# relu(h)² on ScalarE in place of VectorE, and the first w2 tiles in the first product's weight pool

## The chip, the cores and the metric

The kernel runs on one core of one Trainium2 chip. The metric is the device time of one execution in microseconds (us). Five engines work side by side, each through its own instructions in order: TensorE (PE in the profile; PEld is its weight load), VectorE (DVE), ScalarE (ACT), GpSimd (POOL) and SyncE (SP), whose queue issues nearly all DMAs of the part that matters here.

## The reference, cut to what matters

One encoder layer on x of 2048 tokens x 1024: differential attention and a retention scan, mixed into x, then a feed-forward part with a hidden width of 4096.

```
h = rms_norm(x, norm2_g)
u = relu(h @ w_mlp1)          # 2048 x 1024 @ 1024 x 4096
x = x + (u * u) @ w_mlp2      # 2048 x 4096 @ 4096 x 1024
```

Everything ahead of these three lines is the same in both kernels.

## The kernel before, in words

Both ff products are cut into 2 x 2 blocks and computed with seven block products in place of eight (Strassen-Winograd): sums and differences of blocks are formed first, and the results are added up afterwards. Each fp32 operand is split into a high and a low part (`split_sbuf`: the high part by a ScalarE copy on L44, the low part by a VectorE subtraction on L50), and each product is three matmuls, L36 high·high, L37 and L38 with one low part each (`mm3`).

**First ff product.** It goes over two halves of the tokens (`g`), and in each over eight blocks of the hidden width (`blk`). One block (`winograd_block`) runs its seven products in the order b11, b21, t2, t1, t3, b22, t4 (named after the token operand, which lies in SBUF for the whole half). One product is 24 matmuls into two banks `ps`, one for each `s`, so a block is 168 matmuls. The weight side is a raw w1 tile, or a sum of such tiles made by GpSimd on L238 (`comb`, tag `s`, three buffers in pool `wp`): s2 for the product t2, s1 for t1, s3 for t3, s4 for b22. s2 is made from s1. Their splits are `wh` and `wl`, three buffers each. VectorE adds the banks up on L279 into tiles `c`, and each finished tile goes to `consume`: relu(h)² on L1419, a store to DRAM on L1413 (`put`), and from each four tiles four sums on GpSimd (L1417, `comb` inside `consume`), eight a block, which are stored too. In the first half, blocks 1 to 4 are each followed by `fill_units`, which turns and splits a quarter of the second half's tokens: here blocks 2 to 5 run beside that work, and they are called fill blocks below.

**Second ff product.** Seven products p1, p2, p6, p7, p5, p3, p4 follow, each of eight chunks; a chunk is 48 matmuls into eight banks `p`. A chunk needs `ra` (the stored hidden units, L1490, split into `ah` and `al`) and a w2 tile (`br`, 512 KB, L1464, split into `wh` and `wl`). The w2 tiles lie in pool `bp` ("m2b"), four buffers. The pools of this stage (`ap`, `bp`, `cpool`) are opened when the pool `hp` of the first stage is closed, and lie in its place, in the order in which they are opened; a tile there can be loaded when what lay there has been read for the last time.

**What sets the order.** The program is written out for one stage after the other, and a scheduler with a timeline of its own puts each engine's instructions in order at build time. So a change in one place can move instructions on all engines. A DMA on SP whose wait isn't over holds up all that stand behind it on SP.

Of the kernel before, what the change touches and what calls it, by code (L numbers as in the profile page):

```python
# [8 lines left out]
F32 = mybir.dt.float32  # L9
F32R = mybir.dt.float32r  # L10
F16 = mybir.dt.float16
AF = mybir.ActivationFunctionType
ALU = mybir.AluOpType
# [4 lines left out]
P = 128  # L18
# [58 lines left out]
H = G // 2  # L77
# [12 lines left out]
def winograd_units(nc, pool, saved=None, units=UNITS, issued=None, places=None):  # L90

    tb = {n: [pool.tile([P, 4, H], F32R, tag=f"{n}{hl}", name=f"{n}{hl}", bufs=1) for hl in "hl"] for n in places or units}
    if saved is not None:
        for n in units:
            for t, d in zip(tb[n], saved[n]):
                e = nc.gpsimd if issued is not None and n in ("t1",) else nc.sync
                ins = e.dma_start(t[:].bitcast(F32), d[:].rearrange("p (k t) -> p k t", k=4).bitcast(F32))
                if issued is not None:
                    issued.append(ins)
    return tb  # L100
# [424 lines left out]
def pool(tc, name, bufs, space=None, side=None):  # L525
    kw = {} if space is None else dict(space=space)
    return tc.tile_pool(name=name, bufs=bufs, side=side, reuse_waits="tile", **kw)
# [3 lines left out]
def encoder(ctx: ExitStack, tc: tile.TileContext, a: dict, out: bass.AP, dbg=None):  # L531
    nc = tc.nc
    x, w_in, w_out, w1, w2 = a["x"], a["w_in"], a["w_out"], a["w_mlp1"], a["w_mlp2"]
    x = x.rearrange("b s d -> (b s) d")
    out = out.rearrange("b s d -> (b s) d")
# [110 lines left out]
    def load_half(pool, w, c):  # L646
        r = pool.tile([P, KT, 256], F32, tag="raw", name="raw")
        nc.sync.dma_start(r[:], w[:, c : c + 256].rearrange("(k p) n -> p k n", p=P))
        return [r]

    def load_w(pool, w, c0):

        return [r for fh in range(2) for r in load_half(pool, w, c0 + fh * 256)]
# [7 lines left out]
    with ExitStack() as ph:  # L661
        wp = ph.enter_context(pool(tc, "wst", 3))
# [93 lines left out]
        first = load_w(wp, w_in, blocks[0][1] * 512)  # L756
# [117 lines left out]
        for g in range(S // G):  # L874
            if g:
                first = load_w(wp, w_in, blocks[0][1] * 512)
# [276 lines left out]
    with ExitStack() as ph:  # L1153
# [50 lines left out]
        for i in range(LT, NI):  # L1204
# [20 lines left out]
            if i == NI - 4:  # L1225
# [4 lines left out]
                for n in ("vh", "vl"):  # L1230
                    t = ap2.tile([P, 2, DM], F32, tag=n, name="wos")
# [59 lines left out]
    with ExitStack() as ph:  # L1291
# [5 lines left out]
        t = ep.tile([P, 2, DM], F32, tag="raw", name="wos")  # L1297
# [46 lines left out]
        for i in range(NT + 2):  # L1344
# [6 lines left out]
            if i == 12:  # L1351
                first = [r for fh in range(2) for r in load_half(ep, w1, fh * (DFF // 2))]
                tb0 |= winograd_units(nc, ep, saved[1], UNITS[1:2])
                t = ep.tile([P, 2, 4, 256], F32R, tag="raw", name="w0")
# [16 lines left out]
    wp = mlp.enter_context(pool(tc, "m1w", 3))  # L1371
    pp = mlp.enter_context(pool(tc, "ps_m1", 8, PSUM))

    def load_w1(blk):
        return [r for fh in range(2) for r in load_half(ep, w1, fh * (DFF // 2) + blk * 256)]

    with ExitStack() as ph:
        hp = ph.enter_context(pool(tc, "h2T", 1))
        for g in range(S // G):
            if g:  # L1380
                first = load_w1(0)
                tb0 = winograd_units(nc, ep, saved[2], UNITS[:2])
            loads = []
            tb = tb0 | winograd_units(nc, hp, saved[1 + g], UNITS[2:], loads, ("t4", "b22", "t3", "t2", "t1"))
            for blk in range(DFF // 512):
                if ahead:
                    hl = [wp.tile([P, 4, 256], F32R, tag=f"w{n}", name=f"w{n}") for n in "hl"]
                    split_sbuf(nc, hl[0][:], hl[1][:], first[0][:, 4:8], "act", "dve")
                    ahead["a12"] = hl
                    sums = [wp.tile([P, 4, 256], F32, tag="s", name="s") for _ in range(2)]  # L1390
                    nc.gpsimd.tensor_tensor(out=sums[0][:], in0=first[1][:, 0:4], in1=first[1][:, 4:8], op=ALU.add)
                    nc.gpsimd.tensor_tensor(out=sums[1][:], in0=sums[0][:], in1=first[0][:, 0:4], op=ALU.subtract)
                    hl = [wp.tile([P, 4, 256], F32R, tag=f"w{n}", name=f"w{n}") for n in "hl"]
                    split_sbuf(nc, hl[0][:], hl[1][:], sums[1][:], "act", "dve")
                    ahead["s2"] = hl
                    sums = dict(s1=sums[0][:], s2=sums[1][:])
                else:
                    sums = {}
                if blk == 0:
                    raws = first  # L1400
                elif blk == 1:
                    with tc.issue_after(loads[-1].ins):
                        raws = load_w1(blk)
                else:
                    raws = load_w1(blk)

                us = [{} for _ in range(2)]

                def consume(t, fh, th, s):
                    u, f0 = us[s], blk * 256 + s * P  # L1410

                    def put(n):
                        nc.sync.dma_start(ua_d[n][f0 : f0 + P, g * H : (g + 1) * H], u[n][:])  # L1413

                    def comb(n, x0, x1, op, o=None):
                        u[n] = wp.tile([P, H], F32, tag="d", name="c", bufs=BUFS["d"]) if o is None else o
                        nc.gpsimd.tensor_tensor(out=u[n][:], in0=u[x0][:], in1=u[x1][:], op=op)  # L1417

                    nc.vector.scalar_tensor_tensor(  # L1419
                        out=t[:], in0=t[:], scalar=0.0, in1=t[:], op0=ALU.max, op1=ALU.mult  # L1420
                    )
                    n = f"a{th + 1}{fh + 1}"
                    u[n] = t
                    if n == "a21":
                        comb("s1", "a21", "a22", ALU.add)
                        put("s1")
                        comb("s3", "a11", "a21", ALU.subtract, t)
                        put("s3")
                        comb("s2", "s1", "a11", ALU.subtract)
                        put("s2")  # L1430
                    else:
                        put(n)
                    if n == "a12":
                        comb("s4", "a12", "s2", ALU.subtract)
                        put("s4")

                winograd_block(
                    nc, wp, pp, raws, tb, False, consume, [[], []], ahead=ahead, sums=sums, ptag="d"
                )
                ahead = {}  # L1440
                if g == 0 and 0 < blk < 5:
                    x2 = ep.tile([P, 2, DM], F32, tag="raw", name="x2")
                    for i in range(2):
                        r0 = (7 + 4 * i + blk) * P
                        nc.sync.dma_start(x2[:, i], x1n_d[r0 : r0 + P, :])
                    fill_units(
                        nc, pp, wp, ("d", "s"), turn_pair(nc, (x2[:, 0], x2[:, 1]), g2, ident),
                        into_dram(nc, wp, "d", saved[2], blk - 1),
                    )

    with ExitStack() as ph:
        ap = ph.enter_context(pool(tc, "m2a", 1))
        bp = ph.enter_context(pool(tc, "m2b", 4))
        cpool = ph.enter_context(pool(tc, "m2c", 16))
        NC2 = DFF // 2 // 256
        B = {f"b{i + 1}{j + 1}": w2[i * (DFF // 2) : (i + 1) * (DFF // 2), j * 512 : j * 512 + 512] for i in range(2) for j in range(2)}
        HOMES = (("b11h", "b11l"), ("b21h", "b21l"), None)
        count = 0  # L1460

        def load_b(src, c):
            t = bp.tile([P, 2, H], F32, tag="br", name="br")
            nc.sync.dma_start(t[:], src[c * 256 : c * 256 + 256, :].rearrange("(f p) n -> p f n", p=P))  # L1464
            return t

        def part_b(n, c):

            if n in B:
                return load_b(B[n], c)  # L1470
            t = wp.tile([P, 2, H], F32, tag="s", name=n)

            def sub(x0, x1):
                nc.gpsimd.tensor_tensor(out=t[:], in0=x0[:], in1=x1[:], op=ALU.subtract)  # L1474

            if n in ("t1", "t2"):
                sub(load_b(B["b12"], c), load_b(B["b11"], c))
                if n == "t2":
                    sub(load_b(B["b22"], c), t)
                    nc.sync.dma_start(t2_d[c * 256 : c * 256 + 256, :].rearrange("(f p) n -> p f n", p=P), t[:])  # L1480
            elif n == "t3":
                sub(load_b(B["b22"], c), load_b(B["b12"], c))
            else:
                sub(load_b(t2_d, c), load_b(B["b21"], c))
            return t
# [104 lines left out]
```

## Time and profile before

| what | value |
|---|---|
| time, median of 3 runs | 2875.31 us (2872.67 to 2880.72) |
| the profiled execution | 2880.86 us |
| its span, first to last instruction | 2879.1 us |
| mean granted TensorE clock | 0.975 |
| PE busy | 2737.0 us, 95% |
| VectorE, GpSimd, ScalarE busy | 72%, 49%, 39% |

The span is what the trace shows; 1.8 us of the profiled execution lie around it. Times in views are microseconds from the span's start. A matmul is pipelined: at full clock one starts each 0.23 us and is shown as lasting 0.39 us, and at the lower of the clock's two levels one starts each 0.43 us and lasts 0.63 us. Numbers in brackets behind an instruction are the idle time of its engine ahead of it and what ended it.

### The profile page before, as it was taken

The page shows a single profiled execution, that of the slowest core. Times are in us where ns is not written, and L with a number is a line of the kernel's source. Part 1 is how long each engine was busy: PE and PEld are TensorE (multiplying, and loading weights), DVE is VectorE, ACT ScalarE, POOL GpSimd, SP SyncE. Part 2 cuts the span into 40 slices and gives each one's busy share as a digit, 9 for nine tenths or more (in the row PEclk, how much of TensorE's full clock was granted, in tenths as well). Part 3 has the DMA queues.
Part 4 walks back from the last instruction along what each step waited for, and adds up shares of the span by engine and source line. Part 5 has one row for each costly group of instructions (what it writes and reads, how often), then busy time and mean ns, then how long its engine had stood idle before and what let it go on. Part 6 is the DMA issues. An engine that isn't in the chain of part 4 may idle for free. (4 is left out here: it accounts for less than half of the span.)

```text
span 2879.1 us, 40880 instructions
## 1 busy us (share of the span) xinstructions
PE 2737.0 (95%) x15488; PEld 2343.8 (81%) x15488; DVE 2078.5 (72%) x2997; ACT 1133.9 (39%) x1570; POOL 1412.0 (49%) x802
## 2 busy tenths in 40 slices
PE   5998899998889999999899998999999899999999
PEld 4898889997768888888777777788888688888887
DVE  7879754686779998998888499986888534435442
ACT  5334322343457777777433122222222232222221
POOL 6265322513357787787444457666667103323320
PEclk8999999998899999999999999999999999999999
DMA  3466673259433223131487767657444757855461
GB/s 125 150 196 181 225 287 110 92 178 261 115 83 82 66 67 85 55 97 47 157 251 241 273 198 232 203 220 284 157 161 144 276 186 264 302 196 173 165 241 44
DMA packets 361027, 494.48 MB, mean 172 GB/s; under 512 B 23168, under 2 KB 257152, under 8 KB 352640
## 3 DMA queue, kind: packets, MB, share of 16 engines
q1 hardware_dynamic: 338608, 466.71, 49.6%
q10 hardware_dynamic: 21648, 20.98, 2.1%
q0 software_dynamic: 576, 4.19, 0.3%
q8 instruction: 122, 2.00, 0.3%
q14 instruction: 73, 0.60, 0.1%
HBM read 315.64 MB, written 176.16 MB: 171 GB/s over the span
## 5 line engine op out<-in xcount | busy, mean ns | idle before, releaser
L36 PE MATMUL p<-wh,ah 128*128 128x512 f32 x896 | 349.1, 391 | 11.4 <-ACT wh L44 11.4
L37 PE MATMUL p<-wl,ah 128*128 128x512 f32 x896 | 348.8, 389 | 0.0
L238 POOL TENSOR_TENSOR s<-raw 128x1024 f32<-128x1024 f32 x58 | 155.2, 2675 | 335.4 <-DVE wl L50 102.2
L1007 POOL TENSOR_TENSOR p<-p 128x1024 f32<-128x1024 f32 x127 | 303.4, 2412 | 0.1
L1417 POOL TENSOR_TENSOR c<-c 128x512 f32<-128x512 f32 x128 | 218.9, 1733 | 147.6 <-DVE c L1419 145.3
L279 DVE TENSOR_TENSOR c<-ps,c 128x512 f32<-128x512 f32 x360 | 239.3, 684 | 67.8 <-PE ps L38 65.9
L44 ACT ACTIVATE ah<-ra 128x1024 fp32r<-128x1024 f32 x112 | 112.6, 1052 | 429.8 <-PE p L37 412.0
L50 DVE TENSOR_TENSOR wl<-s,wh 128x1024 fp32r<-128x1024 f32 x120 | 189.2, 1590 | 121.9 <-ACT wh L44 115.8
L991 ACT ACTIVATE p<-p,nm 128x2048 f32<-128x2048 f32 x128 | 256.9, 2007 | 33.1 <-DVE nm L979 31.8
L50 DVE TENSOR_TENSOR ah<-ra,ah 128x1024 fp32r<-128x1024 f32 x76 | 106.6, 1438 | 223.3 <-ACT ah L44 223.3
L44 ACT ACTIVATE wh<-s 128x1024 fp32r<-128x1024 f32 x120 | 123.9, 1055 | 320.3 <-POOL s L238 171.6
L1474 POOL TENSOR_TENSOR t<-br 128x1024 f32<-128x1024 f32 x32 | 77.3, 2414 | 347.1 <-DMA br<-in_w_mlp 184.5
L38 PE MATMUL p<-wh,ah 128*128 128x512 f32 x608 | 236.8, 389 | 0.0
L1006 POOL TENSOR_SCALAR p<-p,ratio 128x1024 f32<-128x1024 f32 x127 | 141.8, 1129 | 141.5 <-DVE ratio L1001 106.3
L974 PE MATMUL sc<-ka,qa 128*128 128x512 f32 x512 | 207.2, 405 | 3.5 <-DVE nm L979 3.5
L36 PEld LDWEIGHTS p<-wh,ah 128*128 128x128 f32 x896 | 169.3, 189 | 47.0 <-ACT wh L44 11.8
L44 ACT ACTIVATE wh<-raw 128x1024 fp32r<-128x1024 f32 x89 | 94.4, 1060 | 283.6 <-PE ps L37 186.7
L975 PE MATMUL sc<-ka,qb 128*128 128x512 f32 x512 | 202.5, 396 | 0.0
L37 PEld LDWEIGHTS p<-wl,ah 128*128 128x128 f32 x896 | 168.4, 188 | 35.0
L979 DVE CUSTOM_DVE_ANT_0 p<-sc,bias,nm 128x1024 f32<-128x1024 f32 (+1 forms) x136 | 167.7, 1233 | 23.2 <-PE sc L975 21.2
L55 ACT ACTIVATE aTh<-pa 128x512 fp32r<-128x512 f32 x256 | 151.2, 591 | 83.9 <-PE pa L1168 82.7
L1168 PEld LDWEIGHTS pa<-ident,p 128*128 128x128 f32 x1024 | 120.4, 141 | 63.6 <-issue 26.0
(388 smaller groups left out, 8293.0 us busy)
## 6 DMA issues: line engine op xcount, KB each, us to landing
br<-in_w_mlp SPq DMA_DIRECT2D x88, 512.0 KB, 5.6
raw<-in_w_mlp SPq DMA_DIRECT2D x32, 1024.0 KB, 5.9
raw<-in_w_in SPq DMA_DIRECT2D x28, 1024.0 KB, 5.5
xt<-in_x SPq DMA_DIRECT2D x20, 512.0 KB, 5.6
q<-rqd SPq DMA_DIRECT2D x16, 512.0 KB, 10.9
qa<-qhd SPq DMA_DIRECT2D x64, 128.0 KB, 3.0
qb<-qld SPq DMA_DIRECT2D x64, 128.0 KB, 3.0
ua11d<-c SPq DMA_DIRECT2D x32, 256.0 KB, 2.8
```

Source lines behind the costliest of these rows:

```text
L36: nc.tensor.matmul(out, ah, bh, start=first, stop=False)
L37: nc.tensor.matmul(out, ah, bl, start=False, stop=False)
L38: nc.tensor.matmul(out, al, bh, start=False, stop=last)
L44: nc.scalar.activation(hi, src, AF.Copy)
L50: e.tensor_tensor(out=lo, in0=src, in1=hi.bitcast(F32), op=ALU.subtract)
L279: nc.vector.tensor_tensor(out=o[:], in0=x0[:], in1=x1[:], op=op)
L974: nc.tensor.matmul(sc[:, o : o + 512], qa[:, c, ql], r, start=True, stop=False)
L975: nc.tensor.matmul(sc[:, o : o + 512], qb[:, c, ql], r, start=False, stop=True)
L979: nc.vector.tensor_tensor_reduce(out=p[:, k0 : k0 + w], in0=sc[:], in1=bias[:, b0 : b0 + w], scale=1.0, scalar=nm[:, n - 1 : n] if n else ...
L991: nc.scalar.activation(p[:], p[:], AF.Exp, bias=nm[:, n : n + 1], scale=-1.0, accum_out=l[:])
L1007: e.tensor_tensor(out=p0, in0=p0, in1=p1, op=ALU.add)
L1417: nc.gpsimd.tensor_tensor(out=u[n][:], in0=u[x0][:], in1=u[x1][:], op=op)
```

## The change

Two edits. In `consume`, the one VectorE instruction for relu(h)² becomes two ScalarE activations, Relu and then Square, both in place. In the second ff product, the w2 tiles of p1 (operand b11) are placed in pool `wp`, tag `s` (three buffers, those of the first product's weight sums), and `cpool` is opened ahead of `ap` and `bp`, so that these two lie further on in the place of `hp`.

```
-                    nc.vector.scalar_tensor_tensor(
-                        out=t[:], in0=t[:], scalar=0.0, in1=t[:], op0=ALU.max, op1=ALU.mult
-                    )
+                    nc.scalar.activation(t[:], t[:], AF.Relu)
+                    nc.scalar.activation(t[:], t[:], AF.Square)
...
+        cpool = ph.enter_context(pool(tc, "m2c", 16))
         ap = ph.enter_context(pool(tc, "m2a", 1))
         bp = ph.enter_context(pool(tc, "m2b", 4))
-        cpool = ph.enter_context(pool(tc, "m2c", 16))
...
-        def load_b(src, c):
-            t = bp.tile([P, 2, H], F32, tag="br", name="br")
+        def load_b(src, c, first=False):
+            t = wp.tile([P, 2, H], F32, tag="s", name="br") if first else bp.tile([P, 2, H], F32, tag="br", name="br")
...
             if n in B:
-                return load_b(B[n], c)
+                return load_b(B[n], c, n == "b11")
```

The hp tiles lie in the order t4, b22, t3, t2, t1 (high and low part, 8 KB a partition each). Before, `ap` (16 KB) lay over t4 and `bp` (16 KB) over b22; now `cpool` (32 KB) lies over these two, `ap` over t3 and `bp` over t2.

SP's queue around the end of the first ff product, before. `ra` and `br` are the loads of the second product, `ua` and `us` the stores of the first one's last block.

```order
L1490 DMA ra<-ua11d 128x2x1024 x3
L1413 DMA ua11d<-c 128x512 x2
L1490 DMA ra<-ua11d 128x2x1024
L1413 DMA ua22d<-c 128x512 x2
L1413 DMA us1d<-c 128x512
L1413 DMA us3d<-c 128x512
L1413 DMA us2d<-c 128x512
L1413 DMA us1d<-c 128x512
L1413 DMA ua12d<-c 128x512
L1464 DMA br<-in_w_mlp 128x2x512
```

The same place now (L1490 has become L1491, and L1464 L1465):

```order
L1491 DMA ra<-ua11d 128x2x1024
L1465 DMA br<-in_w_mlp 128x2x512
L1491 DMA ra<-ua11d 128x2x1024
L1465 DMA br<-in_w_mlp 128x2x512
L1491 DMA ra<-ua11d 128x2x1024
L1413 DMA ua11d<-c 128x512
L1465 DMA br<-in_w_mlp 128x2x512
L1413 DMA ua11d<-c 128x512
L1491 DMA ra<-ua11d 128x2x1024
L1413 DMA ua22d<-c 128x512 x2
L1465 DMA br<-in_w_mlp 128x2x512
```

The first w2 load stood behind the last block's stores of sums; now three stand ahead of all stores of ua22 and of the sums.

ScalarE's order in a fill block, from the copies of the bank of the product b11 (L284) to the next block's fill work (`d`), before:

```order
L284 ACTIVATE c<-ps 128x512 x2
L44 ACTIVATE wh<-s 128x1024 x2
L44 ACTIVATE wh<-raw 128x1024 x3
L44 ACTIVATE d_18515<-usrc 128x512
L44 ACTIVATE d_18527<-udif 128x512
L44 ACTIVATE wh<-s 128x1024 x2
```

And the first rows of the same place now (L1419 is Relu, L1420 Square):

```order
L284 ACTIVATE c<-ps 128x512 x2
L1419 ACTIVATE c<-c 128x512
L1420 ACTIVATE c<-c 128x512
L44 ACTIVATE wh<-s 128x1024 x2
L1419 ACTIVATE c<-c 128x512
L1420 ACTIVATE c<-c 128x512
L44 ACTIVATE wh<-raw 128x1024
L1419 ACTIVATE c<-c 128x512
L1420 ACTIVATE c<-c 128x512
L44 ACTIVATE wh<-raw 128x1024
```

A pair of Relu and Square stands ahead of the two splits for the products t3 and b22, and further pairs stand between the raw splits.

GpSimd's order where block 0 of the first half passes into block 1, before (L1417 are the eight sums of block 0, `s<-raw` and `s<-s,raw` the sums s1 and s2 for block 1):

```order
L1417 TENSOR_TENSOR c<-c 128x512 x4
L238 TENSOR_TENSOR s<-raw 128x1024
L1417 TENSOR_TENSOR c<-c 128x512 x3
L238 TENSOR_TENSOR s<-s,raw 128x1024
L1417 TENSOR_TENSOR c<-c 128x512
```

And now:

```order
L1417 TENSOR_TENSOR c<-c 128x512 x6
L238 TENSOR_TENSOR s<-raw 128x1024
L1417 TENSOR_TENSOR c<-c 128x512 x2
L238 TENSOR_TENSOR s<-s,raw 128x1024
L238 TENSOR_TENSOR s<-raw,s 128x1024
```

All eight sums stand ahead of s2 now, where there were seven.

## Rows read from the trace of the kernel before

**Rows 1.** The page: busy us by engine, share of the span, instructions.
```profile
PE 2737.0 (95%) x15488; PEld 2343.8 (81%) x15488; DVE 2078.5 (72%) x2997; ACT 1133.9 (39%) x1570; POOL 1412.0 (49%) x802
```
**Rows 2.** Stretches: us, busy time (count) by engine, granted clock, DMA share, GB/s.
```profile
1777.70:1824.94 47.24, 42.14 (x187) 34.22 (x186) 43.61 (x42) 11.00 (x14) 31.10 (x18) 0.96 0.71 223
2060.82:2098.90 38.08, 38.08 (x169) 31.53 (x168) 31.93 (x31) 8.41 (x9) 27.16 (x13) 1.00 0.44 152
2268.20:2875.20 607.00, 606.96 (x2678) 502.24 (x2676) 253.71 (x224) 161.61 (x168) 138.03 (x64) 1.00 0.57 202
```
**Rows 3.** Waits of PE, 1560 to 2300 us: total, times, longest.
```profile
PE ps L36 <- ACT wh L44: 18.4, 6, 4.5
PE p L36 <- ACT wh L44: 11.4, 1, 11.4
PE ps L38 <- DVE wl L50: 4.4, 5, 2.1
```
**Rows 4.** PE in order of time at the passage: start, duration, instruction.
```profile
2247.81 0.39 PE L36 MATMUL ps<-t4h,wh 128*128 128x512 f32 x1
...
2251.66 0.39 PE L38 MATMUL ps<-t4h,wl 128*128 128x512 f32 x1
2263.44 3.78 PE L36 MATMUL p<-wh,ah 128*128 128x512 f32 x8 [11.39 <-ACT wh L44]
...
2268.19 0.39 PE L37 MATMUL p<-wl,ah 128*128 128x512 f32 x1
```
**Rows 5.** The chain through the passage: start, us, what.
```profile
2252.72 3.39 POOL c L1417 x2
...
2256.54 0.38 SPq L1413
2257.04 5.20 DMA br<-in_w_mlp
2262.33 1.07 ACT wh L44
```
**Rows 6.** SP and VectorE in order of time, shortly before the passage.
```profile
2229.32 9.37 SPq L1490 DMA_DIRECT2D ra<-ua11d  x3
...
2240.02 1.22 DVE L50 TENSOR_TENSOR wl<-s,wh 128x1024 fp32r<-128x1024 f32 x1
```
**Rows 7.** Groups by form, 1600 to 2262 us: busy, mean ns, idle before.
```profile
L1419 DVE SCALAR_TENSOR_TENSOR c<-c 128x512 f32<-128x512 f32 x128 | 135.5, 1059 | 2.7
L279 DVE TENSOR_TENSOR c<-ps,c 128x512 f32<-128x512 f32 x192 | 127.4, 683 | 7.5 <-PE ps L38 6.5
L44 ACT ACTIVATE d<-usrc 128x512 fp32r<-128x512 f32 x16 | 9.1, 619 | 31.8 <-DVE usrc L144 31.8
```
**Rows 8.** Line L1417: duration in ns, min/median/max.
```profile
L1417 POOL TENSOR_TENSOR c<-c x128: 1257/1627/2287, 1637.7 to 2261.7; 128x512 f32<-128x512 f32 x128
```
**Rows 9.** GpSimd and ScalarE in order of time, a fill block's sums.
```profile
1771.54 13.30 POOL L1417 TENSOR_TENSOR c<-c 128x512 f32<-128x512 f32 x8 [15.28 <-DVE c L1419]
...
1789.45 2.78 POOL L238 TENSOR_TENSOR s<-s,raw 128x1024 f32<-128x1024 f32 x1
...
1792.26 2.00 ACT L44 ACTIVATE wh<-s 128x1024 fp32r<-128x1024 f32 x2 [6.15 <-POOL s L238]
```
**Rows 10.** ScalarE, VectorE and PE in order of time, a fill block's product t3.
```profile
1756.29 2.01 ACT L44 ACTIVATE wh<-s 128x1024 fp32r<-128x1024 f32 x2 [6.72 <-POOL s L238]
...
1756.74 1.41 DVE L279 TENSOR_TENSOR c<-ps,c 128x512 f32<-128x512 f32 x2
...
1758.60 0.39 PE L36 MATMUL ps<-t3h,wh 128*128 128x512 f32 x1
...
1761.38 0.50 PE L38 MATMUL ps<-t3h,wl 128*128 128x512 f32 x1 [0.81 <-DVE wl L50]
```
**Rows 11.** VectorE and PE in order of time, second half, the product t3.
```profile
2153.49 1.23 DVE L50 TENSOR_TENSOR wl<-s,wh 128x1024 fp32r<-128x1024 f32 x1 [5.88 <-PE ps L38]
...
2158.74 0.39 PE L36 MATMUL ps<-t3h,wh 128*128 128x512 f32 x1
```

## The prediction

> **What bounds the kernel now.** I read the page first: PE is busy for 95% of the span [rows 1], so an edit pays only where PE stands still or runs at its lower clock. The stretches show where that is. A block of the second half takes 38.08 us with PE busy throughout, and the second ff product runs 607 us without a gap, both at a granted clock of 1.00; a fill block takes 47.24 us, with VectorE busy for 43.61 of them [rows 2]. The waits of PE over the first product and the passage to the second then name three things: 18.4 us in six waits for a `wh`, 4.4 us in five for a `wl`, and one wait of 11.4 us at the passage [rows 3]. All later work of PE follows that last one without a pause, so what is taken from it moves the end.
>
> The chain through the passage says what made it [rows 5]: GpSimd's last sums, then a store on SP that waited for them, then the w2 load `br` issued at 2257.04, 5.20 us of transfer, and 1.07 us of split. In the order before, the load stands behind the stores of the sums, and its place in `hp` is that of b22, which PE reads until about 5.4 us before the end of the product t4. So place and queue together kept it back.
>
> **The passage.** The product t4 ends with the matmul at 2251.66. At full clock a matmul starts each 0.227 us (from 2247.81 to 2251.66 there are 17 steps). The first eight matmuls after the gap take 3.78 us, at the lower of the clock's two levels (1.2 in place of 2.4 GHz), and the twelfth is the one at 2268.19 [rows 4]. Twelve steps at full rate are 2.7 us; the trace shows 16.53. So the passage costs 13.8 us: 11.4 of waiting and 2.4 of low clock and start.
>
> What is late next, once the load stands ahead of those stores? The first w2 tile needs a buffer `s`, which s2 of the last block has left long before; it now follows the load `ra` that went out at 2229.32 [rows 6], so it lands at about 2229.7 + 5.2 = 2235. Its split needs the `wh` buffer of t3, free when t3 ends. In the last block t3 ends at 2251.66 - 48 x 0.227 = 2240.8. Split, low part and a Relu and Square pair ahead of it (about 3.6 us: 1.06 + 1.22 + 1.3) end by 2245, 7 us before PE asks. The second tile needs the buffer of s4, read last by the subtraction at 2240.02 [rows 6]: issue at 2241.3, landed at 2246.5, wanted one chunk after the first, at 2252 + 48 x 0.227 = 2263. The third comes a chunk later again. `ap` now lies over t3 and is free before t4 ends. The w2 tiles of p2 wait in `bp`, over t2, free earlier still. I find nothing within 7 us of PE's need, and take the whole 13.8 us as gained. Bounds: 0 (a load that keeps its old place) and 13.8.
>
> On SP the w2 loads now stand ahead of the last stores, and a load that waits for its buffer holds these up by a chunk or two (11 us each). They are read in p2 or later, behind 8 x 48 x 0.227 = 87 us of p1, so this costs nothing. Beyond the passage PE has no wait to shorten.
>
> **relu(h)² itself.** VectorE loses 128 instructions of 1059 ns, 135.5 us; ScalarE gains 256 of the size of the copy `d<-usrc`, 619 ns [rows 7], about 158 us. ScalarE is busy for 8.4 of 38 us in a block of the second half [rows 2]; the change adds 16 x 0.62 = 9.9 and leaves half of it idle. What counts is order: a Relu waits for VectorE's sum, and the splits queued behind it wait too.
>
> In the second half that stays hidden. The low part for t3 is ready at 2153.49 + 1.23 = 2154.7, and PE asks at 2158.74 [rows 11]; 4 us of cover against a pair of 1.3 us. Cost 0; if the cover were gone it would be 1.3 us a block.
>
> In a fill block the cover isn't there. Now a pair stands ahead of the two splits for t3 and b22. It needs the second of the sums at 1756.74, done at 1758.15; the pair ends at 1759.4 and the two splits at 1760.4 and 1761.4, where they ended at 1758.3 and PE began t3 at 1758.60 [rows 10]. PE's first matmuls of t3 and b22, eight of them, then reach to about 1762.3; the first with a low part ran at 1761.38. That is 0.9 us lost a block.
>
> Against it stands the start of the next block. PE waits there for s2, and s2 comes after the eight sums: GpSimd works without a pause from 1771.54, 13.30 us of sums, s1, fill work, s2 from 1789.45, and the split at 1792.26 [rows 9]. The eight sums could take 8 x 1.257 = 10.1 us [rows 8], so 3.2 us are stretch. VectorE's L1419, with both inputs in SBUF, is stretched too (1059 ns on average), while L279, with one input in PSUM, isn't (683 ns) [rows 7]. About a quarter of VectorE's time beside these sums is L1419, so I give back a quarter of 3.2, 0.8 us a block; the bounds are 0 and 3.2. The sums start no sooner: VectorE's sum, the wait behind a raw split, and a pair of 1.3 us bring the finished tile at about the same time as before.
>
> The Trainium skill states a cause for this in "GPSIMD Engine Reference", section "Specifications": GpSimd's SBUF interfaces are shared with VectorE, and VectorE instructions with two SBUF inputs contend for them. The rows agree with it; by that rule alone the relief would go on to the rival C below.
>
> Four fill blocks: 4 x (0.9 - 0.8) = +0.4 us. At the passage from block 0 to block 1 the order puts one more sum of 1.26 to 1.73 us ahead of s2, where PE already waited, against the same relief: +0.8. Together about +1 us, with bounds from the parts: -13 (all 3.2 us given back in each of four blocks) and +13 (no relief, 0.9 us in each of four blocks, and the 2.4 us of low clock that the passage shows after each new gap).
>
> **The sum.** -13.8 + 1.2 = -12.6 us on the profiled execution's 2880.86, or 2868.3. That execution lies 5.55 us above the median of the runs, 2875.31; the same difference from the median gives 2862.7, and I say 2863.
>
> **Rivals.** A: *the passage stays closed for another reason.* A w2 tile, a `wh` buffer or a bank is late, and the wait at the passage shrinks to some 5 us with the low clock behind it. For it: seven things must be ready at once, and only one was visible as the last. Against: the 7 us of cover found above. Time: 5 + 2.4 remain, so -13.8 + 7.4 + 1.2 = -5, about 2870.
>
> B: *ScalarE's queue becomes the bound, and the kernel is slower.* One pass over 512 elements on VectorE becomes two on ScalarE, each split of a weight sum stands behind a Relu that waits for VectorE, and PE waits for the split. For it: 18.4 us of PE's waits already name `wh` [rows 3]. Against: 4 us of cover in the blocks that aren't fill blocks. It decides from where the delay of the splits passes that cover: with 1.5 us of wait in each of the 12 blocks without fill work and 3 in the other four, 18 + 12 - 13.8 gives +16, about 2891.
>
> The skill's rule "relu, max, min, add, mul: use VectorE, not ScalarE" ("ScalarE: Activation LUTs", section "Rules for kernel authors") speaks for B. The rows show 1238 ns on ScalarE for 1059 on VectorE, so by engine time alone the rule holds here; by its advice the first edit should cost, and the time would be nearer to B's.
>
> C: *the fill blocks gain as well.* With 135.5 us off VectorE and the whole stretch off GpSimd's sums, the wait for s2 falls by 2.5 us in each of four blocks, and the low clock behind the shorter gap by 1 us. For it: VectorE is 92% busy there [rows 2]. Against: the t3 splits now stand behind the pair [rows 10]. Time: -13.8 - 4 x 3.5 = -28, about 2847.
>
> D: *the loads don't come earlier.* The order shows them moved; only the relu edit would then count: 2876.
>
> **How the numbers follow.** The forecast has 0.60, A 0.16, B 0.07, C 0.14, D 0.03. A measurement of this kernel tells 0.3% (8.6 us) from no change, so below 2866.7 is faster. The forecast's own range is 2855 to 2870: five parts in six of it are faster, 0.50, and 0.10 the same. C is faster. A splits, a quarter faster and the rest the same; D is the same; B is slower but for a small part. Faster 0.68, same 0.25, slower 0.07. The range that leaves out about 0.1 on either side is 2848 to 2874: it holds the forecast, nearly all of A and the near half of C; it leaves out B.
>
> **What would show it.** In the profile after: no wait of PE for `wh` between `ps` and `p` and a granted clock of 1.00 through the passage; `br` loads issued from about 2230; no PE wait in the second half's blocks (this is where B would show); in fill blocks a new wait of about 2 us ahead of t3's first matmul and a wait ahead of t2 smaller by about 1 us. A passage still over 3 us, or fill blocks longer than 48 or shorter than 44 us, would make the prediction wrong.

## The result, and the profile after

The changed kernel takes 2858.89 us (median of 4 runs, 2854.20 to 2862.14), the kernel before 2876.37 (4 runs, 2872.67 to 2880.72): ratio 0.9937, 95% interval 0.9917 to 0.9957. The time said was 2863, from 2848 to 2874.

The page after begins like this (busy us by engine, share of the span, instructions):

```profile
span 2857.1 us, 41084 instructions
PE 2731.3 (96%) x15488; PEld 2338.9 (82%) x15488; DVE 1953.1 (68%) x2869; ACT 1287.6 (45%) x1826; POOL 1374.2 (48%) x802
```

Against [rows 1], VectorE has 125 us less, ScalarE 154 more, and GpSimd 38 less, although nothing was taken from GpSimd. PE has 5.7 us less for the same matmuls: it stood less at its lower clock.

**The passage.** The waits of PE from 1560 to 2300 us, answering [rows 3], and PE's timeline where the first product ends, answering [rows 4]:

```profile
PE ps L36 <- ACT wh L44: 18.3, 10, 2.5
PE ps L38 <- DVE wl L50: 3.9, 4, 2.1
```

```profile
2243.50 0.39 PE L38 MATMUL ps<-t4h,wl 128*128 128x512 f32 x1
2243.72 0.39 PE L36 MATMUL p<-wh,ah 128*128 128x512 f32 x1
2243.95 0.39 PE L37 MATMUL p<-wl,ah 128*128 128x512 f32 x1
```

There is no wait on `p` any more, and no matmul of 0.63 us behind it: `p` follows `ps` after 0.22 us, where 11.78 lay between them [rows 4]. SP's timeline shows why; the first three w2 loads go out here, and not behind the sums as in [rows 5]:

```profile
2215.53 0.38 SPq L1465 DMA_DIRECT2D br<-in_w_mlp  x1
...
2218.93 0.37 SPq L1465 DMA_DIRECT2D br<-in_w_mlp  x1
...
2225.84 0.39 SPq L1465 DMA_DIRECT2D br<-in_w_mlp  x1
```

**The two kinds of block.** Stretches of a fill block and of a second-half block, and the second product, answering [rows 2]:

```profile
1772.45:1818.55 46.10, 42.15 (x187) 33.94 (x185) 36.64 (x34) 20.30 (x31) 29.87 (x18) 0.96 0.72 229
2060.00:2098.08 38.08, 38.08 (x170) 31.53 (x169) 22.73 (x22) 18.20 (x26) 21.66 (x13) 1.00 0.43 152
2249.00:2856.00 607.00, 604.16 (x2666) 499.96 (x2664) 252.75 (x224) 161.25 (x167) 140.46 (x66) 1.00 0.58 204
```

These blocks (6 to 15, called second-half blocks here and in the texts below) take 38.08 us each from first matmul to first matmul, as before, with ScalarE busy for 18.20 us in place of 8.41. Groups by form between 1595 and 2250 us, answering [rows 7]:

```profile
L1420 ACT ACTIVATE c<-c 128x512 f32<-128x512 f32 x128 | 80.9, 632 | 4.0
L1419 ACT ACTIVATE c<-c 128x512 f32<-128x512 f32 x128 | 80.2, 626 | 172.7 <-DVE c L279 169.8 <-DMA ua22d<-c 2.9
L279 DVE TENSOR_TENSOR c<-ps,c 128x512 f32<-128x512 f32 x192 | 128.2, 687 | 83.6 <-PE ps L38 80.0 <-DMA us2d<-c 2.0 <-DMA raw<-in_w_mlp 0.6
L1417 POOL TENSOR_TENSOR c<-c 128x512 f32<-128x512 f32 x128 | 194.3, 1543 | 170.8 <-ACT c L1420 153.1 <-DMA ua22d<-c 15.4
```

VectorE's L279 now waits 80 us for PE, where it waited 6.5: VectorE no longer runs behind.

**Where the 22.0 us between the two spans lie**, by the first matmul of each block in PE's timeline. The first ff product starts at 1595.68, before at 1599.90: 4.2 us from unchanged stages (in the profiled executions of all these kernels that start lies between 1589.1 and 1599.9, so it says nothing). Block 0: +0.07 us. Blocks 1 to 5: 227.68 to 224.33, -3.35. Blocks 6 to 15 up to the first `p`: 393.02 to 380.80, -12.22; of it 11.56 are the passage's wait. From the first `p` to the end: 615.66 to 613.38, -2.28, the low clock behind that wait. The changed stages thus give -17.8, and the medians -17.5.

### The profile page after: what moved, and what is told of

The parts are those of the page before. It is cut to its first block, busy times and chain, and to the rows that moved or that the text cites. A ratio compares the mean times of both kernels' runs of the same rounds, so it can differ in the third digit from the quotient of the medians.

```text
span 2857.1 us, 41084 instructions
## 1 busy us (share of the span) xinstructions
PE 2731.3 (96%) x15488; PEld 2338.9 (82%) x15488; DVE 1953.1 (68%) x2869; ACT 1287.6 (45%) x1826; POOL 1374.2 (48%) x802
## 4 chain that ended last, share of the span: by engine, by line
PE 76%; DVE 11%; DMA 5%; POOL 3%; issue 3%; ACT 2%; SPq 1%; DVEq 0%; ACTq 0%; POOLq 0%
PE ps L37 11%; PE ps L38 11%; PE ps L36 11%; PE p L38 7%; PE p L36 7%; PE p L37 7%; PE pa L1168 4%; PE sc L974 4%; PE sc L975 4%; PE po L36 2%; PE po L38 2%; PE po L37 2%; DMA mixd<-yt 1%; DVE wl L50 1%; POOL s L238 1%
## 5 line engine op out<-in xcount | busy, mean ns | idle before, releaser
L36 PE MATMUL p<-wh,ah 128*128 128x512 f32 x896 | 348.4, 389 | 0.0
L279 DVE TENSOR_TENSOR c<-ps,c 128x512 f32<-128x512 f32 x360 | 240.0, 686 | 142.6 <-PE ps L38 138.1
L238 POOL TENSOR_TENSOR s<-raw 128x1024 f32<-128x1024 f32 x58 | 149.2, 2573 | 334.6 <-DVE wl L50 119.6
L50 DVE TENSOR_TENSOR wl<-s,wh 128x1024 fp32r<-128x1024 f32 x120 | 196.1, 1641 | 132.2 <-ACT wh L44 132.0
L1417 POOL TENSOR_TENSOR c<-c 128x512 f32<-128x512 f32 x128 | 194.3, 1543 | 170.8 <-ACT c L1420 153.1
L50 DVE TENSOR_TENSOR ah<-ra,ah 128x1024 fp32r<-128x1024 f32 x76 | 103.0, 1390 | 219.3 <-ACT ah L44 219.3
L36 PEld LDWEIGHTS p<-wh,ah 128*128 128x128 f32 x896 | 168.2, 188 | 34.9
L56 DVE TENSOR_TENSOR aTl<-pa,aTh 128x512 fp32r<-128x512 f32 x256 | 170.1, 686 | 1.6 <-DMA vh<-vhd 0.8
```

The lines of the kernel that those rows point to most:

```text
L36: nc.tensor.matmul(out, ah, bh, start=first, stop=False)
L50: e.tensor_tensor(out=lo, in0=src, in1=hi.bitcast(F32), op=ALU.subtract)
L279: nc.vector.tensor_tensor(out=o[:], in0=x0[:], in1=x1[:], op=op)
```

## The experiments

Times are medians; ratios are to the kernel before, with their 95% intervals. "Passage" is the time from the start of the last `ps` matmul to that of the first `p`; "blocks 2 to 5" the sum of these fill blocks; the last column the mean of GpSimd's 128 sums. These three are from each kernel's one profiled execution.

| kernel | us (runs) | ratio | passage, us | blocks 2 to 5, us | sums, ns |
|---|---|---|---|---|---|
| before | 2876.37 (4) | 1 | 11.78 | 185.69 | 1733 |
| changed | 2858.89 (4) | 0.9937 [0.9917, 0.9957] | 0.22 | 182.29 | 1543 |
| e1 relu edit alone | 2869.40 (12) | 0.9982 [0.9973, 0.9991] | 6.65 | 187.10 | 1526 |
| e2 pool edits alone | 2861.86 (6) | 0.9956 [0.9940, 0.9971] | 0.23 | 185.67 | 1751 |
| e3 relu, order of pools | 2868.63 (12) | 0.9984 [0.9974, 0.9993] | 6.80 | 182.34 | 1529 |
| e4 relu, weight pool | 2862.74 (6) | 0.9948 [0.9933, 0.9964] | 0.23 | 187.24 | 1546 |
| e5 a11 on VectorE | 2854.99 (5) | 0.9928 [0.9915, 0.9940] | 0.22 | 180.98 | 1547 |
| e6 three Relu | 2862.96 (4) | 0.9953 [0.9937, 0.9970] | 0.23 | 190.56 | 1508 |
| e7 five Relu | 2903.15 (4) | 1.0096 [1.0082, 1.0110] | 0.22 | 220.57 | 1582 |
| e10 Relu on VectorE | 2857.55 (4) | 0.9943 [0.9927, 0.9960] | 0.22 | 183.37 | 1624 |
| e11 the same, two inputs | 2877.40 (10) | 1.0007 [0.9997, 1.0016] | 0.23 | 191.11 | 1777 |
| e12 changed, again | 2856.52 (3) | 0.9940 [0.9908, 0.9971] | 0.23 | 183.91 | 1544 |

The theory at the start: the passage was closed by the pool edits, through the place of the w2 tiles and SP's order together, and relu(h)² is about free. Rivals: one of the two pool edits does it alone, or the relu edit has a share.

**e1: the relu edit alone** (L1419 of before replaced by Relu and Square, the pools as before).

> Relu and Square on ScalarE, the pools as before. Theory (the w2 loads earn the time, relu(h)^2 only a little in the fill blocks): PE's wait at the passage stays between 9 and 13 us with low clock behind it, the five blocks with or before fill work are 3 us shorter in total, time 0.999 of before (2873). Rival (the first edit earns it, since ScalarE finishes the last block's stores earlier and the loads follow): the wait at the passage falls under 5 us, time 0.994 to 0.996.

The wait at the passage is 6.3 us, between the theory's 9 to 13 and the rival's 5. Blocks 1 to 5 took 229.1 us against 227.7 before, where 3 us less was expected. The timelines of GpSimd's last sums, of SP and of PE's first `p`:

```profile
2240.51 12.16 POOL L1417 TENSOR_TENSOR c<-c 128x512 f32<-128x512 f32 x8 [23.44 <-ACT c L1420]
...
2246.11 0.38 SPq L1413 DMA_DIRECT2D ua12d<-c  x1
2246.59 0.41 SPq L1463 DMA_DIRECT2D br<-in_w_mlp  x1
...
2252.80 3.78 PE L36 MATMUL p<-wh,ah 128*128 128x512 f32 x8 [6.26 <-ACT wh L44]
```

In the kernel before, the same sums:

```profile
2249.77 13.18 POOL L1417 TENSOR_TENSOR c<-c 128x512 f32<-128x512 f32 x8 [20.48 <-DVE c L1419]
```

The load still stands behind the stores of the sums, but the eight sums begin 5.6 us ahead of the last `ps` matmul (2246.15), where it was 1.9 before (2249.77 against 2251.66), and so the load goes out 5 us earlier against the end of t4. Of these 5 us, 3.7 are the earlier start and 1.2 the sums themselves, which reach the awaited store in 5.2 us in place of 6.4. What came late in the kernel before was VectorE: with L1419 off it, the last block's tiles are finished sooner. This share of the passage the prediction had put at nothing. That low clock still follows the wait shows in the 3.78 us for eight matmuls.

**e2: the pool edits alone** (the change without its first edit).

> relu(h)^2 in one VectorE instruction as before, the w2 tiles of p1 in the weight pool and cpool opened first. Theory: the passage has no wait and no low clock, the fill blocks keep their waits of 3 to 4.5 us for t2 with low clock behind them, time 0.995 of before (2862). Rival (first edit earns it): 0.999.

The passage closes with relu(h)² still on VectorE. The fill blocks and GpSimd's sums stay as before (185.67 us, 1751 ns), so the shorter sums belong to the relu edit; whether the fill blocks gain by it the later runs leave open. VectorE's lag shows in another place: the last block takes 40.07 us, with one wait of 1.69 for a `wl`. The gains of e1 (0.18%) and e2 (0.44%) come to 0.62%, the changed kernel's to 0.63%, but they don't add up place by place: e1's 5 us at the passage are contained in what e2 gains there. Beside the pool edits the relu edit gives 2.0 us in the last block (40.07 to 38.08). The medians of e2 and of the changed kernel are 3.0 us apart, and their intervals overlap.

**e3 and e4: the two pool edits one at a time**, both with the relu edit.

```
# e3: cpool stands first, and no tile moves to the weight pool
-                return load_b(B[n], c, n == "b11")
+                return load_b(B[n], c)
# e4: p1's tiles in the weight pool, and cpool last as before
-        cpool = ph.enter_context(pool(tc, "m2c", 16))
         ap = ph.enter_context(pool(tc, "m2a", 1))
         bp = ph.enter_context(pool(tc, "m2b", 4))
+        cpool = ph.enter_context(pool(tc, "m2c", 16))
```

> After, but the w2 tiles of p1 stay in bp; cpool is opened first, so bp lies over t2. Theory as it was predicted (place in hp and queue held the load back): with bp over t2, free 20 us before t4 ends, the loads could go early, wait under 3 us, 0.994. Rival (the place doesn't matter; the build order, which still shows the first w2 load behind the last block's stores of sums, does): the passage keeps a wait of 9 to 13 us, time 0.998 to 0.999 of before.

> After, but cpool is opened last as before, so ap lies over t4 and bp over b22; the w2 tiles of p1 lie in the weight pool. Theory (only the weight pool matters): no wait at the passage, time as after, 0.994. Rival (the order of the pools is needed too, since the first ah in ap and the p2 loads in bp then stand in the queue until t4 and b22 are read): a wait of 2 to 8 us at the passage or in p1's first three chunks, time 0.996 to 0.998.

e3's wait of PE at the passage, and its first w2 load; then e4's first w2 load:

```profile
PE p L36 <- ACT wh L44: 6.4, 1, 6.4
```

```profile
2246.81 0.41 SPq L1465 DMA_DIRECT2D br<-in_w_mlp  x1
```

```profile
2219.50 0.38 SPq L1464 DMA_DIRECT2D br<-in_w_mlp  x1
```

That wait is e1's 6.3 again, between e3's theory (under 3) and its rival (9 to 13), and the time is the rival's: another place in `hp` brings nothing, since there too the load stands behind the stores of the sums in SP's order and goes out 0.5 us behind the last `ps` matmul (2246.36). In e4 it goes out 28 us ahead of that matmul (2247.45), and the passage closes without the order of the pools. So the weight pool, with the order on SP that comes with it, is what does it, and a change of place in `hp` alone does nothing. No run moves the load up in SP's order and leaves its tile over b22, so whether the order alone would be enough stays open.

**e5: a11 on VectorE**, aimed at the new wait ahead of t3.

```
+                    if n == "a11":
+                        nc.vector.scalar_tensor_tensor(
+                            out=t[:], in0=t[:], scalar=0.0, in1=t[:], op0=ALU.max, op1=ALU.mult
+                        )
+                    else:
                         nc.scalar.activation(t[:], t[:], AF.Relu)
                         nc.scalar.activation(t[:], t[:], AF.Square)
```

> As the changed kernel, but relu(h)^2 of the tile a11 (two of a block's eight tiles, the pair that now stands on ScalarE ahead of the hi copy wh that t3 waits for) is done by VectorE in its one instruction as before; the other six stay on ScalarE. Theory: the new wait of 2.03 us ahead of t3 in each of blocks 2 to 5 is those 2 x 1.25 us on ScalarE; it goes, the blocks 2 to 5 come out 0.5 to 2 us shorter than the changed kernel's 45.69, 46.08, 46.10 and 44.42 us, the passage stays closed, and the time is 2 to 8 us under the changed kernel's (0.991 to 0.993 of the kernel before). Rival: t3 is late through VectorE's own split wl or through PE's low clock, whoever does relu(h)^2; then a wait of about 2 us stays ahead of t3, and the time is the changed kernel's (0.9937) within 2 us, or worse by the 1.06 us instructions that go back to VectorE.

PE's groups in blocks 1 to 5 (busy and mean ns of one, idle time before them), first of before, then of the changed kernel, then of e5:

```profile
L36 PE MATMUL ps<-t2h,wh 128*128 128x512 f32 x40 | 18.3, 458 | 17.8 <-ACT wh L44 17.8
L36 PE MATMUL ps<-t1h,wh 128*128 128x512 f32 x40 | 17.4, 436 | 0.0
L36 PE MATMUL ps<-t3h,wh 128*128 128x512 f32 x40 | 15.6, 390 | 0.0
L38 PE MATMUL ps<-t3h,wl 128*128 128x512 f32 x40 | 15.1, 399 | 1.9 <-DVE wl L50 1.9
```

```profile
L36 PE MATMUL ps<-t2h,wh 128*128 128x512 f32 x40 | 16.9, 423 | 10.7 <-ACT wh L44 10.7
L36 PE MATMUL ps<-t1h,wh 128*128 128x512 f32 x40 | 16.6, 415 | 0.0
L36 PE MATMUL ps<-t3h,wh 128*128 128x512 f32 x40 | 16.0, 400 | 7.0 <-ACT wh L44 7.0
L38 PE MATMUL ps<-t2h,wl 128*128 128x512 f32 x40 | 15.7, 414 | 1.8 <-DVE wl L50 1.8
```

```profile
L36 PE MATMUL ps<-t2h,wh 128*128 128x512 f32 x40 | 17.2, 430 | 13.0 <-ACT wh L44 13.0
L36 PE MATMUL ps<-t3h,wh 128*128 128x512 f32 x40 | 15.7, 392 | 0.0
L38 PE MATMUL ps<-t3h,wl 128*128 128x512 f32 x40 | 15.5, 403 | 2.7 <-DVE wl L50 2.7
```

The wait for `wh` ahead of t3 is gone, so those pairs on ScalarE had caused it. But of its 7.0 us, 2.3 come back at t2, which waits for GpSimd's chain and not for PE, and 2.7 within t3 itself, as waits for VectorE's `wl`, where the changed kernel has none. The fill blocks are 1.3 us shorter together, less than they differ from one execution to the next (below), and the time is 3.9 us less, within the two intervals. e5 has the lowest median of all; that it beats the changed kernel isn't shown.

**e6 and e7: how much of ScalarE's work is hidden.** Relu is idempotent, so more passes change nothing but ScalarE's load.

```
+                    nc.scalar.activation(t[:], t[:], AF.Relu)   # e6: twice more, e7: four times more
                     nc.scalar.activation(t[:], t[:], AF.Relu)
                     nc.scalar.activation(t[:], t[:], AF.Square)
```

> As the changed kernel, with Relu done three times on each tile before Square (four ScalarE passes in place of two; the values are the same), so that 2 x 0.65 = 1.3 us more lie between a tile's sum on VectorE and its use by GpSimd. Theory: a second-half block has PE's operands some 4 us ahead, so these blocks stay at 38.08 us with no PE wait; ScalarE is busy 18.2 + 10.4 = 28.6 of 38. The fill blocks 2 to 5 have no such cover: 1.3 us each at the least (one tile's pair ahead of wh), up to 7 (the stretch of 21 us from t3 on, where ScalarE has 17 us of work already, takes 10.5 more). Passage closed. Together 5 to 28 us over the changed kernel. Rival (ScalarE's queue holds wh back everywhere): the second-half blocks lengthen as well, by 1 us or more each, and the time is over 30 us above the changed kernel's.

> As the changed kernel, with Relu done five times on each tile before Square (six ScalarE passes; the values are the same). ScalarE then has 8.1 + 48 x 0.655 = 39.5 us of work in a second-half block, more than its 38.08. Theory: here ScalarE's queue becomes the bound, as the slower rival of the prediction had it; each of the ten second-half blocks takes 39.5 us or more with PE waits on ACT wh, and the fill blocks 2 to 5 lengthen by 8 to 20 us each; the time is 45 to 110 us above the changed kernel's. Rival: what ScalarE does beside its own chain is free while its work is not far over the block; then the second-half blocks stay within 0.5 us of 38.08 and only the fill blocks lengthen.

With e6 all ten second-half blocks stay at 38.08 us. Blocks 2 to 5 take 8.3 us more and block 1 2.3 less; the time is 4.1 us more, a little under the 5 to 28 expected. With e7 the cover ends; the time is 44.3 us over the changed kernel, just under the 45 to 110 expected. Stretches of a second-half block early in the row and of one late in it, and the waits of PE from 1540 to 2300 us:

```profile
1954.00:1992.08 38.08, 38.08 (x170) 31.55 (x169) 23.09 (x22) 33.50 (x59) 24.61 (x15) 1.00 1.02 404
2089.00:2128.78 39.78, 38.37 (x170) 31.46 (x169) 18.64 (x20) 32.67 (x58) 22.50 (x12) 1.00 0.45 152
```

```profile
PE ps L36 <- ACT wh L44: 52.6, 5, 13.6
PE ps L36 <- ACT c L284: 9.0, 6, 1.9
```

Four blocks still run at 38.08, then five at 39.78 and the last at 40.32. The expected size, 39.5 in all ten, was near for six, its reason not: ScalarE is busy for 33 of 40 us, and PE waits 1.4 us in each of five blocks and 1.9 in the last for ScalarE's copy of a bank (L284) that stands behind the passes. The fill blocks take 38 us more, 9 to 11 each. So the prediction's slower rival exists, and begins somewhere between four and six passes a tile; at two the second half is far from it.

**e8 and e9: is it VectorE's two inputs that stretch GpSimd's sums?** Two idle instructions on a scratch tile of 128x256 behind each tile's Square; their results go nowhere. The lines that make the tile and set it to 0 are left out here.

```
+                    nc.vector.tensor_tensor(out=scr[:], in0=scr[:], in1=scr[:], op=ALU.max)   # e8, twice
+                    nc.vector.tensor_scalar(scr[:], scr[:], 0.0, None, op0=ALU.max)           # e9, twice
```

> As the changed kernel, with idle work for VectorE behind each tile's Square: two maxima of a scratch tile of 128x256 with itself (two inputs from the on-chip memory, as relu(h)^2 on VectorE had; 128 x 2 instructions, whose results nobody reads). GpSimd's sums L1417 took 1733 ns on average in the kernel before and 1543 ns in the changed one. Theory: VectorE's instructions with two such inputs stretch GpSimd's sums beside them; the mean goes back to 1640 ns or more, and the eight sums of a fill block to 12.7 us or more (13.30 before, 12.08 changed). Rival: the sums are longer when VectorE is busier or stands in another order, whatever its instructions read; then this kernel and the one with one input come out within 40 ns of each other.

> As the kernel with two inputs, with the maximum of the same scratch tile and the constant 0 (one input from the on-chip memory) in place of the maximum with itself. Theory: GpSimd's sums stay at the changed kernel's 1543 ns within 40 ns. Rival: they come out as with two inputs.

One run each: 2929.33 and 2903.33 us. These instructions hold up VectorE's chain: PE waits 40.3 and 22.7 us for a `wl`, where it waits 3.9 in the changed kernel. The sums take 1549 and 1510 ns: within 40 ns of each other, as the rival had it, and far from 1733. VectorE's own rows tell more; e8's, then e9's, both while GpSimd is in a row of seven sums (from 1808.73 for 10.85 us, and from 1799.09 for 9.73):

```profile
1808.14 0.43 DVE L1424 TENSOR_TENSOR scr<-scr 128x256 f32<-128x256 f32 x1
...
1810.40 2.31 DVE L50 TENSOR_TENSOR wl<-raw,wh 128x1024 fp32r<-128x1024 f32 x1
...
1815.60 1.40 DVE L1425 TENSOR_TENSOR scr<-scr 128x256 f32<-128x256 f32 x1
1817.03 1.40 DVE L1424 TENSOR_TENSOR scr<-scr 128x256 f32<-128x256 f32 x1
```

```profile
1802.33 0.67 DVE L279 TENSOR_TENSOR c<-c,ps 128x512 f32<-128x512 f32 x1
...
1806.41 1.26 DVE L1425 TENSOR_SCALAR scr<-scr 128x256 f32<-128x256 f32 x1
1807.70 1.27 DVE L1424 TENSOR_SCALAR scr<-scr 128x256 f32<-128x256 f32 x1
1809.00 0.29 DVE L1425 TENSOR_SCALAR scr<-scr 128x256 f32<-128x256 f32 x1
```

An instruction of 0.43 us takes 1.40 beside the sums, one of 0.29 us takes 1.27: about the length of one sum (1.39 us each in e9, 1.55 in e8). L279, which reads a bank, keeps its 0.67. So in these rows both engines take turns by whole instructions, and a scratch tile of half the width was too small a thing to stretch a sum by much. A longer instruction does more: L50, 1.22 us where GpSimd stands still, takes 2.31 here, and the sum beside it 2.25. These two runs left the count of inputs open.

**e10 and e11: the same question on the tile itself.** Relu on VectorE, Square on ScalarE, by an instruction with one input or with two.

```
-                    nc.scalar.activation(t[:], t[:], AF.Relu)
+                    nc.vector.tensor_scalar(t[:], t[:], 0.0, None, op0=ALU.max)                  # e10
+                    nc.vector.scalar_tensor_tensor(out=t[:], in0=t[:], scalar=0.0, in1=t[:],
+                                                   op0=ALU.max, op1=ALU.max)                     # e11
```

> As the changed kernel, with Relu on VectorE (maximum with 0 in place, one input from the on-chip memory) and Square on ScalarE: one pass on each engine. GpSimd's sums L1417 took 1733 ns on average before (relu(h)^2 on VectorE, two inputs), 1751 ns with the new pools alone and 1543 ns in the changed kernel; two idle maxima of a scratch tile beside them brought 1549 (two inputs) and 1510 ns (one). Theory: what stretched them is VectorE's pass over the tile itself with two inputs; here the sums stay at 1510 to 1580 ns. Rival: it is that VectorE, with 8 more passes a block, runs later and so beside them, whatever its inputs; then 1640 ns or more. On the time: theory, the pair ahead of t3's wh is half as long, so the wait there is 1.2 us or less, and the time is the changed kernel's or up to 5 us less; rival, 2 to 5 us more.

> As the kernel with Relu on VectorE, the same value by VectorE's instruction with two inputs (maximum with 0, then maximum with the tile itself), then Square on ScalarE. Theory: GpSimd's sums go to 1640 ns or more here and not in the kernel with one input. Rival: both have the same mean within 40 ns; then the count of inputs doesn't matter.

The groups of VectorE and GpSimd by form, e10's and then e11's:

```profile
L1419 DVE TENSOR_SCALAR c<-c 128x512 f32<-128x512 f32 x128 | 98.0, 766 | 2.7
...
L1417 POOL TENSOR_TENSOR c<-c 128x512 f32<-128x512 f32 x128 | 204.8, 1624 | 160.3 <-ACT c L1420 120.9 <-DMA ua22d<-c 37.2
```

```profile
L1419 DVE SCALAR_TENSOR_TENSOR c<-c 128x512 f32<-128x512 f32 x128 | 122.7, 959 | 2.9
...
L1417 POOL TENSOR_TENSOR c<-c 128x512 f32<-128x512 f32 x128 | 224.4, 1777 | 167.5 <-ACT c L1422 157.4 <-DMA ua22d<-c 7.9
```

e11's expectation holds: its sums take 1777 ns, and e10's stay under 1640. e10's doesn't hold whole: its 1624 lies between its theory and its rival, and the wait ahead of t3 is 0.9 to 1.9 us a block, where 1.2 or less was said. The instruction with two inputs stretches the sums more, by 153 ns, but the one with one input stretches them too, to 1624 from 1543. On the time, e10 is level with the changed kernel and e11 with the kernel before. e11 loses 7.7 us to e10 in blocks 2 to 5, 3.3 in block 1, and 6.9 in the last two blocks, where VectorE is late again (a wait of 3.3 us for a `wl`). So the instruction with two inputs costs, both on VectorE and on GpSimd; that Relu stands on VectorE and not on ScalarE, by one input, changes the time by nothing that these runs show. But the count of inputs isn't all that differs. Where GpSimd stands still, just ahead of a row of sums (from 1758.45 in e10 and 1771.76 in e11), the two instructions take:

```profile
1757.28 0.43 DVE L1419 TENSOR_SCALAR c<-c 128x512 f32<-128x512 f32 x1
```

```profile
1771.00 0.69 DVE L1419 SCALAR_TENSOR_TENSOR c<-c 128x512 f32<-128x512 f32 x1
```

The instruction with two inputs is the longer one by itself, and if the engines take turns by whole instructions, its length could stretch the sums whatever it reads. No run has two instructions of the same length and a different count of inputs on the tile, so this rival stands.

**e12: the changed kernel again**, for the clock in the fill blocks (below).

> The changed kernel once more. In the kernels with the relu edit alone and with the weight pool alone, whose orders of the first ff product are the changed kernel's, the clock fell after the wait ahead of t3 in blocks 3 to 5, and these blocks took 47.7, 47.7 and 46.0 us in place of 46.1, 46.1 and 44.4. Theory: whether it falls there differs from one execution to the next; then this execution may show either, and one with the longer blocks would settle it. Rival: it belongs to the kernel; then blocks 3 to 5 are 46.1, 46.1 and 44.4 us within 0.2 again. Seeing the short blocks again would leave both open.

Here block 3 took 47.69 us and blocks 4 and 5 46.11 and 44.46. From t2 to the next t2, in block 3 and then block 4 of this execution:

```profile
1735.92:1783.62 47.70, 42.48 (x185) 34.02 (x185) 36.74 (x34) 20.41 (x31) 29.89 (x18) 0.96 0.70 221
1783.62:1829.70 46.08, 40.88 (x184) 32.84 (x184) 36.62 (x34) 20.26 (x31) 29.86 (x18) 1.00 0.74 228
```

The first profiled execution of this kernel had 46.08 in block 3. So the longer block belongs to the execution and not to the kernel, as the theory had it.

## Why the prediction was right, and where it wasn't

**The passage, -13.8.** Measured: 11.56 of wait and 2.28 of low clock, 13.84 in all. The bound that was chosen, everything gained, was the right one; nothing was late next: ScalarE's split of the first tile ran at 2232.82, 11 us ahead of PE. The loads went out from 28 us ahead of the end of t4 (2215.53 against 2243.50); 22 were said (2229.7 against 2251.66). The step "place and queue together kept it back" was wrong in its first half: with the load late in the queue the place made no difference, 6.3 us of wait over b22 (e1) and 6.4 over t2 (e3), and e4 closes the passage with the pools where they were before.

**relu(h)² in the second half, cost 0.** Right, by e6 with room to spare. What was missing is a gain: in e1 it took 5.1 us off the passage, because VectorE no longer ran behind and the sums got shorter. The rows for it were there: L279 had waited only 6.5 us for PE [rows 7], which said that VectorE was never ahead. For the same reason the text's time for rival D, 2876 with the relu edit alone, was too high: 2869.40.

**The fill blocks, +0.4 in four blocks, and +0.8 at block 1.** The two mechanisms are there, both larger than they were costed. The new wait ahead of t3 is 7.0 us in all (1.5 to 2.0 a block, as the last part of the prediction said; its sum had 0.9 a block, the later start of PE alone). GpSimd's eight sums went from 13.30 us [rows 9] to this in the changed kernel:

```profile
1765.38 12.08 POOL L1417 TENSOR_TENSOR c<-c 128x512 f32<-128x512 f32 x8 [15.34 <-ACT c L1420]
```

That is 1.2 us a block in place of 0.8, and the wait ahead of t2 fell by 7.1 us, since what PE loses at t3 it need not wait at t2: that wait ends when GpSimd is done. The waits before and after come to the same, 19.7 and 19.5 us with those for `wl`. The -3.35 us of the profile are the clock: the matmuls of t2 and t1 at 0.63 us were fewer (mean of t2's L36 458 ns before, 423 after). And that part changes from one execution to the next: with the same order of the first product, blocks 2 to 5 took 182.29, 182.34, 183.91, 187.10 and 187.24 us (changed, e3, e12, e1, e4), against 185.69 before. So the sign of this term isn't settled; between -3.4 and +1.6 it lies inside the bounds of -13 to +13, and by itself can't be told from nothing. That the first profile shows -3.4 is in part the luck of that execution. Block 1 cost 0.05 where 0.8 was said.

**The sum.** -12.6 was said, -17.8 measured in the changed stages: -13.8 as forecast, -3.3 in place of +1.2, and -0.7 in the last block, where a wait for `wl` went with VectorE's lag. The forecast came near by its largest term, the passage; the terms of the fill blocks and of the last block were missed, and both are small against its range.

**The rivals.** A: the passage is wholly closed, so no. B: no wait of PE in the second half, and the relu edit alone made the kernel no slower (e1); e7 is the kernel in which it happens. C: its gain was to come from the wait for s2 and the clock behind it, 3.5 us a block; in the first profile it was 0.85, with the blocks between the 44 and 48 us that were said. D: the loads came earlier.

**The rule on inputs.** By e10 and e11 an instruction of VectorE with two inputs costs 20 us more in time than one with one input that does the same; how much of it is contention and how much the instruction's own length (0.69 us against 0.43) isn't shown. The Trainium skill's "GPSIMD Engine Reference", section "Specifications", names contention for VectorE's instructions with two inputs and for those in a 2-port mode, and "SBUF — State Buffer", section "SBUF: two separate sides", says that the port pair is locked for a whole instruction. e9's instruction of 0.29 us that takes 1.27 beside a sum agrees; no run here shows which mode it was in.

## What to carry to other kernels

Ask of a wait at a passage which transfer is late and what stands ahead of it in its queue; a place in memory that looks like the cause can be tried apart from the order, and here it did nothing. An engine whose waits for its producer are near zero runs behind, and taking work off it can pay wherever its last result is awaited, also far from the edited line. Split a difference of two profiles by stage before explaining it: here 4.2 of 22.0 us lay in stages that nobody had changed.

## What the runs showed of the hardware

The clock did not fall after the same wait each time. After the same wait of 2.03 us ahead of t3 in block 3, PE went on at full clock in the changed kernel's first profile and fell to the lower level (0.63 us a matmul) in e12, the same kernel; one fall costs such a block 1.6 us. VectorE and GpSimd took turns by whole instructions where both worked on the on-chip memory: 0.29 us became 1.27, and 0.43 became 1.40 (e9, e8), while instructions of VectorE that read a bank kept their 0.67. ScalarE's passes that don't wait for one another started 0.52 us apart in e7; a pair on the same tile started 0.66 apart in the changed kernel.
